# Two-layer hybrid attention block on one core: the second layer's output product as groups of seven products of sums

## The chip, the cores and the metric

The kernel runs on one core of one Trainium2 chip. The metric is the time of one execution on the device, in microseconds (us). The engines of the core are named as the profile names them: PE (TensorE, matrix products; PEld is its loading of the stationary operand, which overlaps PE), DVE (VectorE), ACT (ScalarE), POOL (GpSimd) and SP (SyncE, here only a queue that starts transfers). Every engine takes its own instructions in order and waits at one whose inputs are not there yet.

## The reference

The model has two layers (DEPTH = 2) over 512 tokens of 1024 features, with 16 meta tokens in front (T = 528). Each layer normalizes, projects, runs a sparse attention branch and a pooling branch, and joins both with gates. What matters here is the end of a layer:

```python
y_a = jnp.einsum('bte,ed->btd', attn * jax.nn.silu(gate_a), w_a)
...
y_b = jnp.einsum('bte,ed->btd', pooled * jax.nn.silu(gate_b), w_b)
g_a, g_b = jnp.split(jax.nn.sigmoid(merge), 2, axis=-1)
return x + jnp.einsum('btd,de->bte', g_a * y_a + g_b * y_b, w_out)
...
return h[:, N_META:]
```

The last line of the layer is the output product: the merged features (528 x 1024) times w_out (1024 x 1024), plus the residual x. Of the second layer only the 512 tokens behind the meta tokens are returned, so its product is 512 x 1024 x 1024.

## The kernel before

**Layout.** Activations lie features by tokens: 128 features of a stripe on the partitions, eight stripes j = 0 to 7, tokens along the free axis. Token t = 1 to 4 of the list TOK means tokens 16 to 143, 144 to 271, 272 to 399 and 400 to 527. Every float32 matrix operand is split into a high part (a cast to the reduced type float32r) and a low part (the remainder), and a product is made of three: high by high, high by low, low by high. So a cast, mostly on ACT, and a subtraction, on DVE or POOL, stand before each operand.

**Weights.** The list `chunks` (lines 114 to 131) gives the weight matrices in the order of their use, in pieces. A raw chunk is loaded by SP into two tiles (`raw`, four buffers, so two chunks lie there at a time). A plain chunk is split by `high` and `low` (lines 194 to 202): two casts of 128x1024 on ACT and two subtractions of that size on DVE. `w_load` in `low` starts the load of the next chunk, whose transfers wait for the tiles to be free.

**Groups of seven products.** The chunks named in `mixed` (lines 128 and 243 to 305) are used otherwise: ten chunks of w_in per layer in `mix_gates` (line 959). There the product of 256 output features with 1024 input features by two token halves is not eight block products but seven, of sums of blocks, by a scheme of the Strassen and Winograd kind. The weights' sums need two DVE operations of 128x512 (s2, and s2 minus a11) and two transfers on POOL's queue that add one tile to another (`first_sum` in line 239, and a12 plus s2 in line 266); after that come seven casts and seven subtractions of 128x512. The sums of the activations are made once for all ten (`sums_of_h`). Each product is 12 matmuls of 128x256. Its results are put together from PSUM banks U, S and X with copies on ACT (`out`) and sums on DVE (`total`).

**Around the output product, second layer.** First comes the attention branch's product with w_a (lines 1284 to 1304): for each stripe j, two halves of tokens, 12 matmuls each into one of three PSUM banks `d`. DVE then makes the merged value in place (`ta[j]`): one operation that multiplies the gate with the bank, which frees it, and one that adds the other branch (`zb`). ACT casts it to `hhi`, and POOL subtracts to get `hlo` (stripe 7: DVE). At the same time DVE and ACT split the first chunk of w_out.

Then comes the output product (lines 1360 to 1381): four chunks of 256 output features by four tiles of 128 tokens, sixteen groups. Each group transposes the residual `RES` (two transposes on PE, copied by ACT to `rt`), makes 24 matmuls with tokens as the rows of the result, and DVE adds half the product to `rt` and gives `ot`, which SP stores. In the very first group the three matmuls of k = 7 stand last (line 1374), since stripe 7 is the last to be ready.

**Order.** PE and DVE run in the order in which the program writes them; `later(fn, n)` puts work off until n groups of matmuls have been issued. ACT, POOL and SP are ordered by a scheduler. `prep_one` takes the next step of weight preparation from a queue, one for each group that is done.

Of the kernel before, what the change touches and what calls it, by code (L numbers as in the profile page):

```python
# [8 lines left out]
F32 = mybir.dt.float32  # L9
# [6 lines left out]
D = 1024  # L16
# [74 lines left out]
def tile_block(ctx: ExitStack, tc: tile.TileContext, x, meta, w_in, pool_w, w_a, w_b, w_out, rows, hgain, c_tab, out):  # L91
# [864 lines left out]
    ROLES = [(0, 1, 2), (2, 0, 1), (1, 2, 0)]  # L956
    NEEDS = {"a11": 2, "a12": 2, "s2": 4, "s1": 5, "s3": 6, "s4": 7, "a22": 8}

    def mix_gates(sa, zb, ta, s0, n2, operands, splits, alos):
        base = popped[0] - progress[W["use"]]  # L960
        for q in range(-2, 8):
            if q == -1:
                share[0] = FULL
            c = W["use"]
            W["use"] += 1
            ops = ready[c]
            w_prep_enqueue()
            bs = [bank("d") for _ in range(3)]
            U, S, X = (bs[r] for r in ROLES[(q + 2) % 3])
            done = [0]  # L970

            def product(ps, name, start):
                while progress[c] <= NEEDS[name]:
                    prep_one()
                B, wt = operands[name], ops[name]
                for k in range(4):
                    for e, (x, y) in enumerate(((0, 0), (0, 1), (1, 0))):
                        pe.matmul(ps[:, :n2], wt[:, x, k], B(y, k), start=start and k == e == 0,
                                  stop=k == 3 and e == 2, skip_group_check=True)

            def end():
                done[0] += 1
                group_done()
                while prep_q and (popped[0] < base + 9 * (q + 2) + LEAD + done[0] * 9 // 7 or (q == 7 and done[0] > 4)):
                    prep_one()

            def gate(eh, t, src, in_sheet):
# [20 lines left out]
                dve.tensor_tensor(o, ps[:, :n2], part, op=OP.add)  # L1008
                gate(eh, t, o, True)

            def out(ps, name):
                o = sheet(n2, name)[:, :n2]
                act.copy(o, ps[:, :n2])
                return o
# [4 lines left out]
            product(U, "a11", True)  # L1019
            p1 = out(U, "p1")  # L1020
            end()
            product(X, "a12", True)
            end()
            product(U, "s2", False)
            u = out(U, "u2")
            total(0, 0, X, p1)
            end()
            product(S, "s1", True)
            p5 = out(S, "p5")
            end()  # L1030
            if q == 7:
                alos()
            product(U, "s3", False)
            total(1, 1, U, p5)
            end()
            product(S, "s4", False)
            total(0, 1, S, u)
            end()
            product(U, "a22", False)
            gate(1, 0, U[:, :n2], False)  # L1040
            end()
            splits()
            ready.pop(c)
            if q == -1:
                later(lambda: SIL.update(ready=True), 4)


    ss0 = one.tile([128, 5], F32, name="ss0")
# [46 lines left out]
    for l in range(2):  # L1095
# [187 lines left out]
        flush()  # L1283
        for c in range(2):
            w = chunk()
            for mi in range(4):
                j = 4 * c + mi
                for hf, a, n, o in (halves if l == 0 else [(0, 16, HB - 16, 0), (1, HB, T - HB, 0)]):
                    ps = dense(w, mi, a, n, (ahi, alo), 4, True)
                    d = ta[j][:, a:a + n]  # L1290
# [66 lines left out]
                    later(lambda: norm_half(1, 0, mm, LAG2), 2)  # L1357
            hooks = {0: lambda: stats(1), 1: lambda: norm_half(1, 1, mm, LAG3)}
        else:
            for c in range(4):  # L1360
                w = chunk()
                for t in range(1, 5):
                    s, m = TOK[t]
# [15 lines left out]
                    dve.scalar_tensor_tensor(ot[:, :256], ps[:, :256], 0.5, rt[:, :256], op0=OP.mult, op1=OP.add)  # L1379
                    nc.sync.dma_start(out[0, s - 16:s + 112, c * 256:(c + 1) * 256], ot[:, :256])  # L1380
                    group_done()


# [50 lines left out]
```

## Time and profile before

| what | value |
|---|---|
| three runs | 753.22, 750.17, 749.46 us, median 750.17 |
| the profiled execution | 753.65 us |
| its span in the profile | 751.9 us |
| granted PE clock over the span | 0.999 |
| first matmul of the output product to the end of the last | 699.71 to 748.52 us |

The span is the time from the first to the last instruction of the profiled execution; the execution itself is 1.75 us longer. Rows of a timeline begin with the start in us from the span's start and the duration in us, then the engine, the line, the operation, the tiles written and read, shapes, and the count where neighbours were merged; in square brackets stands the idle time before and what ended it. Because of a helper that records costs, all PE and DVE instructions carry line 62, so they are told apart by their tiles. Rows of the chain of waits have start, duration, engine and tile. In a table by group the last columns are busy us in all, mean ns of one, and idle us before with its cause.

### The profile page before, as it was taken

What the parts mean: (1) busy time and instruction counts of PE and PEld (TensorE: products, weight loads), DVE (VectorE), ACT (ScalarE), POOL (GpSimd) and SP (SyncE); (2) the same over time, 40 slices, a digit from 0 to 9 for tenths busy, and PEclk for the clock granted to TensorE, in tenths of its full rate; (3) what the DMA queues carried; (4) which work ended last, traced back from release to release, by engine and by line L of the source; (5) the groups of instructions that cost most, each with busy time, mean ns of one, the idle gap of its engine ahead of it and who ended that gap; (6) DMA issues with size and microseconds to landing.
All of it is one profiled execution on the core that took longest, in us unless ns stands there. A gap on an engine that the chain in (4) does not pass through costs nothing.

```text
span 751.9 us, 15957 instructions
## 1 busy us (share of the span) xinstructions
PE 738.9 (98%) x5962; PEld 711.0 (95%) x5962; DVE 575.8 (77%) x1452; ACT 468.3 (62%) x1061; POOL 241.9 (32%) x312
## 2 busy tenths in 40 slices
PE   8999999999999999999999999999999999999998
PEld 7999999999999999999999989998899999999998
DVE  5876898998998865794359668999989986668531
ACT  5768745657887875543245886557588887754320
POOL 2652174621222130163256401755022221205100
PEclk9999999999999999999999999999999999999999
DMA  7666674864563444633422776669354643435411
GB/s 261 213 160 166 161 164 114 205 162 99 120 133 86 97 107 107 195 131 117 139 87 85 192 187 164 166 152 233 77 122 117 137 104 94 112 108 192 140 44 43
DMA packets 99277, 103.26 MB, mean 137 GB/s; under 512 B 4816, under 2 KB 80368, under 8 KB 99200
## 3 DMA queue, kind: packets, MB, share of 16 engines
q1 hardware_dynamic: 88752, 74.89, 32.6%
q0 software_dynamic: 10368, 27.27, 19.7%
q8 instruction: 47, 0.77, 0.4%
q14 instruction: 30, 0.25, 0.1%
q10 hardware_dynamic: 80, 0.08, 0.1%
HBM read 66.41 MB, written 8.55 MB: 100 GB/s over the span
## 4 chain that ended last, share of the span: by engine, by line
PE 85%; DVE 9%; ACT 3%; DMA 1%; issue 1%; POOL 0%; SPq 0%; DVEq 0%; POOLq 0%; ACTq 0%
PE d L62 69%; PE a L62 11%; PE v L62 4%; DVE w L62 3%; DVE lt L62 1%; DVE sc L62 1%; DVE s L62 1%; DVE c L62 1%; DMA xt<-in_x_dram 1%; DVE sila L62 1%; DMA raw<-s 1%; ACT lt L764 1%; ACT w L253 1%; DVE zb L62 1%; DVE m L62 0%
## 5 line engine op out<-in xcount | busy, mean ns | idle before, releaser
L62 PE MATMUL d<-hhi,w 128*128 128x256 f32 (+3 forms) x1344 | 268.9, 291 | 1.4 <-DVE w L62 1.4
L62 PEld LDWEIGHTS d<-hhi,w 128*128 128x128 f32 x1344 | 214.3, 188 | 5.2 <-DVE w L62 2.5
L62 PE MATMUL d<-hlo,w 128*128 128x256 f32 (+3 forms) x672 | 182.9, 289 | 0.0
L62 PEld LDWEIGHTS d<-hlo,w 128*128 128x128 f32 x672 | 126.5, 188 | 1.4 <-issue 0.2
L62 DVE TENSOR_TENSOR w<-raw,w 128x512 fp32r<-128x512 f32 (+1 forms) x152 | 123.0, 819 | 2.4 <-ACT w L253 2.2
L62 PE MATMUL d<-w,hhi 128*128 128x256 f32 x768 | 121.9, 287 | 0.3 <-ACT sq L642 0.3
L62 PEld LDWEIGHTS d<-w,hhi 128*128 128x128 f32 x768 | 104.5, 188 | 4.8 <-issue 1.6
L62 PE MATMUL d<-hsum,w 128*128 128x264 f32 (+1 forms) x720 | 96.6, 286 | 1.3 <-DVE w L62 0.9
L62 PEld LDWEIGHTS d<-hsum,w 128*128 128x128 f32 x720 | 90.0, 188 | 2.2 <-DVE w L62 1.1
L253 ACT CAST w<-raw 128x512 fp32r<-128x512 f32 x120 | 69.6, 621 | 10.0 <-DVE raw L62 6.5
L62 PE MATMUL d<-w,hlo 128*128 128x256 f32 x384 | 72.4, 281 | 0.0
L62 PEld LDWEIGHTS d<-w,hlo 128*128 128x128 f32 x384 | 57.0, 188 | 0.0
L62 DVE MATCH_REPLACE8 sc<-m,sc 128x400 f32<-128x400 f32 (+2 forms) x100 | 54.3, 549 | 0.0
L62 DVE MAX8 m<-sc 128x8 f32<-128x400 f32 (+2 forms) x100 | 52.7, 557 | 0.9
L211 POOL DMA_DIRECT2D w<-raw x32 | 29.6, 942 | 69.8 <-ACT w L210 48.1
L241 POOL DMA_DIRECT2D raw<-raw x20 | 18.0, 901 | 101.7 <-DMA raw<-in_w_in_dram 31.7
L779 POOL TENSOR_SCALAR pm<-lt,rs 128x16 f32<-128x16 f32 x48 | 29.4, 661 | 63.7 <-DVE rs L62 59.4
L764 ACT ACTIVATE lt<-lt,mn,NR 128x144 f32<-128x144 f32 (+3 forms) x64 | 42.2, 662 | 8.8 <-DVE mn L62 8.7
L62 DVE SCALAR_TENSOR_TENSOR sc<-r,wsg,sc 128x144 f32<-128x144 f32 (+3 forms) x56 | 32.4, 581 | 17.1 <-ACT r L688 14.9
L62 PE MATMUL d<-mhi,w 128*128 128x272 f32 (+2 forms) x192 | 45.3, 324 | 0.0
L1295 POOL TENSOR_TENSOR hlo<-ta,hhi 128x256 fp32r<-128x256 f32 (+1 forms) x28 | 28.2, 1021 | 45.7 <-PE d L62 33.2
L651 POOL TENSOR_TENSOR t<-t,t 128x256 f32<-128x256 f32 (+1 forms) x34 | 32.4, 954 | 27.5 <-DVE t L62 26.2
(224 smaller groups left out, 1449.9 us busy)
## 6 DMA issues: line engine op xcount, KB each, us to landing
raw<-in_w_in_dram SPq DMA_DIRECT2D x88, 256.0 KB, 3.3
raw<-in_w_in_dram SPq DMA_DIRECT2D x32, 512.0 KB, 4.2
w<-raw POOLq DMA_DIRECT2D x32, 512.0 KB, 5.4
raw<-in_w_out_dram SPq DMA_DIRECT2D x16, 512.0 KB, 3.3
raw<-raw POOLq DMA_DIRECT2D x20, 256.0 KB, 4.6
raw<-s POOLq DMA_DIRECT2D x20, 256.0 KB, 3.3
kept<-res SPq DMA_DIRECT2D x16, 264.0 KB, 3.5
res<-kept SPq DMA_DIRECT2D x16, 264.0 KB, 5.8
```

Source lines behind the costliest of these rows:

```text
L62: return fn(*a, **k)
L211: gp.dma_start(t, raws[c][s], accum_op=OP.add)
L241: gp.dma_start(raws[c][0][:, 1], raws[c][0][:, 0], accum_op=OP.add)
L253: act.copy(t[:, 0], blk[src[n]])
L651: added[0] = gp.tensor_tensor(t1[:m, :256], t1[:m, :256], t2[:m, :256], op=OP.add).ins
L764: act.activation(L[hh][:, :n], L[hh][:, :n], AF.Exp, scale=NR[:, i, h:h + 1], bias=mn[:, hh:hh + 1], accum_out=sm[:, hh:hh + 1])
L779: (gp if j < 3 else dve).tensor_scalar(pms[i][:, 2 * j + hh, :], L[hh][:, 0:16], rs[:, hh:hh + 1], None, op0=OP.mult)
L1295: pool_end = gp.tensor_sub(hlo[:, j, a:a + n], d, f(hhi[:, j, a:a + n]))
```

## The change

The first of the second layer's four output chunks stays as it was. The other three are put into `mixed` and go through groups of seven products, 256 output features by 512 tokens each, features by tokens. The body of `mix_gates` becomes a function of its own, `group_of_products`, with the same order of products.

The sums of the merged activations are made in `sums_of_merged` while the last four stripes of the w_a product are computed: for each pair (k, k + 4) `first` as soon as the loop comes to stripe 4 + k, `sums` two groups later, and `lows` and `fourth` three groups later. They work in place in `ta`, with the tiles t1 (osum1), t2 (osum2) and t3 (osum3) for the high and low parts; the low part of t1 is POOL's. The last sum takes the place of the second token half of `hhi` and `hlo` for stripes 0 to 3 (`last_high`, `last_low`), after the first output chunk has read them.

The results are added to the residual in place, features by tokens, and `turned_out` transposes each 128 features by 256 tokens to token rows, copies them on ACT and stores them, two products later.

```diff
+    mixed |= set(range(len(chunks) - 3, len(chunks)))
...
             if s == 1:
                 del raws[c]
                 w_load()
+                first_sum(c + 1)
...
+    def group_of_products(r, base, n2, operands, total, direct, mid=None):
...
+        product(U, "a11", True)
+        p1 = out(U, "p1")
+        end()
+        product(X, "a12", True)
+        end()
+        product(U, "s2", False)
+        u = out(U, "u2")
+        total(0, 0, X, p1)
+        end()
+        product(S, "s1", True)
+        p5 = out(S, "p5")
+        end()
+        if mid:
+            mid()
+        product(U, "s3", False)
+        total(1, 1, U, p5)
+        end()
+        product(S, "s4", False)
+        total(0, 1, S, u)
+        end()
+        product(U, "a22", False)
+        direct(1, 0, U[:, :n2])
+        end()
+        ready.pop(c)
...
+    def sums_of_merged(ta):
+
+        c0, c1 = slice(16, 272), slice(272, 528)
+        t1 = one.tile([128, 2, 4, 256], F32R, tag="D", name="osum1")
...
+        def first(k):
+            a0, a1 = ta[k][:, c0], ta[k][:, c1]
+            dve.tensor_tensor(a0, a0, a1, op=OP.subtract)
+            act.copy(t1[:, 0, k], a0)
+            gp.tensor_sub(t1[:, 1, k], a0, f(t1[:, 0, k]))
+
+        def sums(k):
+            a0, a1, b1 = ta[k][:, c0], ta[k][:, c1], ta[4 + k][:, c1]
+            dve.tensor_tensor(a1, b1, a1, op=OP.subtract)
+            dve.scalar_tensor_tensor(b1, b1, -1.0, a0, op0=OP.mult, op1=OP.subtract)
+            act.copy(t2[k][:, 0], b1)
+            act.copy(t3[k][:, 0], a1)
+
+        def lows(k):
+            dve.tensor_sub(t2[k][:, 1], ta[4 + k][:, c1], f(t2[k][:, 0]))
+            dve.tensor_sub(t3[k][:, 1], ta[k][:, c1], f(t3[k][:, 0]))
+
+        def fourth(k):
+            b0, b1 = ta[4 + k][:, c0], ta[4 + k][:, c1]
+            dve.scalar_tensor_tensor(b0, b1, -1.0, b0, op0=OP.mult, op1=OP.subtract)
+
+        def last_high(k):
+            act.copy(hhi[:, k, c1], ta[4 + k][:, c0])
+
+        def last_low(k):
+            dve.tensor_sub(hlo[:, k, c1], ta[4 + k][:, c0], f(hhi[:, k, c1]))
...
+    def turned_out(j, t):
+
+        tp = bank("a")
+        for a in range(2):
+            s = 16 + 256 * t + 128 * a
+            pe.transpose(tp[:, 128 * a:128 * a + 128], RES[0][:, j, s:s + 128], ident)
+        ot = tmp.tile([128, HB], F32, tag="tt", name="ot", bufs=6)
+        act.copy(ot[:, :256], tp[:, :256])
+        nc.sync.dma_start(out[0, 256 * t:256 * t + 256, 128 * j:128 * j + 128].rearrange("(a p) e -> p a e", a=2),
+                          ot[:, :256].rearrange("p (a e) -> p a e", a=2))
+
+    def mix_out(operands):
+        base = popped[0] - progress[W["use"]]
+        for q in range(3):
+            def add(eh, t, src):
+                j = 2 + 2 * q + eh
+                d = RES[0][:, j, 16 + 256 * t:272 + 256 * t]
+                dve.scalar_tensor_tensor(d, src, -0.5 if eh else 0.5, d, op0=OP.mult, op1=OP.add)
+                later(lambda: turned_out(j, t), 2)
+
+            def total(eh, t, ps, part):
+                o = sheet(256, "c")[:, :256]
+                dve.tensor_tensor(o, ps[:, :256], part, op=OP.add)
+                add(eh, t, o)
+
+            group_of_products(q, base, 256, operands, total, add)
+        flush()
...
             w = chunk()
+            if l and c:
+                first, sums, lows, fourth, last_high, last_low, operands = sums_of_merged(ta)
             for mi in range(4):
                 j = 4 * c + mi
+                if l and c:
+                    first(mi)
+                    later(lambda k=mi: sums(k), 2)
+                    later(lambda k=mi: (lows(k), fourth(k)), 3)
...
-            for c in range(4):
+            for c in range(1):
                 w = chunk()
...
+            for k in range(4):
+                last_high(k)
+            later(lambda: [last_low(k) for k in range(4)], 1)
+            mix_out(operands)
```

More of the change, by code (lines that the diff above doesn't have):

```diff
@@ L957, in tile_block, with product, end, out @@
     NEEDS = {"a11": 2, "a12": 2, "s2": 4, "s1": 5, "s3": 6, "s4": 7, "a22": 8}
+    def group_of_products(r, base, n2, operands, total, direct, mid=None):
+        c = W["use"]
+        W["use"] += 1
+        ops = ready[c]
+        w_prep_enqueue()
+        bs = [bank("d") for _ in range(3)]
+        U, S, X = (bs[i] for i in ROLES[r % 3])
+        done = [0]
+        def product(ps, name, start):
+            while progress[c] <= NEEDS[name]:
+                prep_one()
+            B, wt = operands[name], ops[name]
+            for k in range(4):
+                for e, (x, y) in enumerate(((0, 0), (0, 1), (1, 0))):
+                    pe.matmul(ps[:, :n2], wt[:, x, k], B(y, k), start=start and k == e == 0,
+                              stop=k == 3 and e == 2, skip_group_check=True)
+        def end():
+            done[0] += 1
+            group_done()
+            while prep_q and (popped[0] < base + 9 * r + LEAD + done[0] * 9 // 7 or (mid and done[0] > 4)):
+                prep_one()
+        def out(ps, name):
+            o = sheet(n2, name)[:, :n2]
+            act.copy(o, ps[:, :n2])
+            return o
+        product(U, "a11", True)
[22 more added lines that the diff above has]
+        ready.pop(c)
     def mix_gates(sa, zb, ta, s0, n2, operands, splits, alos):
@@ L963, in mix_gates, with gate @@
                 share[0] = FULL
[L964 to L987, printed above, removed]
+            def gate(eh, t, src, in_sheet=False):
                 j = 2 * q + eh
@@ L1018, in mix_gates @@
                     ta[j] = tmp.tile([128, T], F32, tag="B", name="ta", bufs=8)
[L1019 to L1041, printed above, removed]
+            group_of_products(q + 2, base, n2, operands, total, gate, alos if q == 7 else None)
             splits()
-            ready.pop(c)
             if q == -1:
                 later(lambda: SIL.update(ready=True), 4)
+    def sums_of_merged(ta):
+        c0, c1 = slice(16, 272), slice(272, 528)
+        t1 = one.tile([128, 2, 4, 256], F32R, tag="D", name="osum1")
+        t2 = [tmp.tile([128, 4, 128], F32R, tag="P", name="osum2", bufs=PB).rearrange("p (s a) c -> p s (a c)", s=2)
+              for _ in range(4)]
+        t3 = [tmp.tile([128, 544], F32R, tag="L", name="osum3", bufs=LB)[:, :512].rearrange("p (s c) -> p s c", s=2)
+              for _ in range(4)]
+        def first(k):
[19 more added lines that the diff above has]
+            dve.tensor_sub(hlo[:, k, c1], ta[4 + k][:, c0], f(hhi[:, k, c1]))
+        operands = {
+            "a11": lambda s, k: H[s][:, k, c0],
+            "a12": lambda s, k: H[s][:, 4 + k, c0],
+            "s4": lambda s, k: H[s][:, 4 + k, c1],
+            "s1": lambda s, k: t1[:, s, k],
+            "s2": lambda s, k: t2[k][:, s],
+            "s3": lambda s, k: t3[k][:, s],
+            "a22": lambda s, k: H[s][:, k, c1],
+        }
+        return first, sums, lows, fourth, last_high, last_low, operands
```

5 lines of the change are left out of this document (1 added, 4 removed).

## The prediction

> **What bounds the kernel now.** I read the page's busy shares first, then its chain, then the chain in order of time over the last 75 us, then the windows and the timelines of VectorE (DVE) and GpSimd (POOL) there.
>
> ```profile
> span 751.9 us, 15957 instructions
> PE 738.9 (98%) x5962; PEld 711.0 (95%) x5962; DVE 575.8 (77%) x1452; ACT 468.3 (62%) x1061; POOL 241.9 (32%) x312
> PE 85%; DVE 9%; ACT 3%; DMA 1%; issue 1%; POOL 0%; SPq 0%; DVEq 0%; POOLq 0%; ACTq 0%
> ```
>
> ```profile
> 647.68 2.85 PE d L62 x24
> ...
> 677.22 22.28 PE d L62 x186
> 699.49 0.22 PE a L62 x2
> 699.71 2.84 PE d L62 x24
> 748.52 0.04 DVEq L62
> ```
>
> TensorE (PE) is the bound. From 677.22 us the chain is PE without a gap: the branch product (w_a) to 699.49, then sixteen groups of the output product, each a pair of transposes (0.22) and 24 matmuls (2.84, so 0.118 each), to 748.52. A matmul taken out saves its 0.118 as long as nothing makes PE wait. The same rate holds in the existing groups of products (24 in 2.85 at 647.68).
>
> ```profile
> 690.00:700.00 10.00, 10.00 (x87) 10.00 (x86) 8.93 (x16) 4.79 (x9) 7.60 (x8) 1.00 0.27 91
> 720.00:730.00 10.00, 10.00 (x87) 10.00 (x86) 2.41 (x4) 2.17 (x4) 0.00 (x0) 1.00 0.12 41
> 740.00:752.00 12.00, 8.51 (x73) 8.29 (x71) 1.27 (x3) 0.74 (x2) 0.00 (x0) 0.94 0.13 45
> ```
>
> The columns are the window, its length, busy time of PE, weight loads, DVE, ACT and POOL, the granted clock, and DMA. Here lies the difficulty. The output product has DVE and POOL nearly free (DVE 2.41 of 10 us), but the new sums start ahead of it, in the second half of the branch product, where DVE is busy 8.93 of 10 us and POOL 7.60.
>
> **The change part by part.** *Matmuls.* Removed are 12 groups of 24 = 288; added are three chunks of seven products of 12 = 252. The 36 fewer are worth 36 x 0.118 = **-4.26 us**. The 24 transposes of these chunks stay, behind the products instead of ahead. Six 128x1024 subtractions on DVE and six casts on ACT go too; they were hidden (2.41 and 2.17 of 10 us busy) and give nothing.
>
> *Sums for the operands.* The merged features lie in eight stripes, j = 0 to 7. For each of four pairs (k and k + 4) DVE gets seven operations of 128x256 with both inputs in SBUF: first 1, sums 2, lows 2, fourth 1, and last_low 1 later. By the order of the instructions eleven of them (four first, two sums pairs, one lows pair, one fourth) come ahead of the update of stripe 7, and DVE takes its queue in order.
>
> ```profile
> 683.65 1.21 DVE L62 TENSOR_TENSOR w<-raw,w 128x1024 fp32r<-128x1024 f32 x1
> 686.12 0.42 DVE L62 TENSOR_TENSOR ta<-ta,zb 128x256 f32<-128x256 f32 x1
> 686.46 1.76 DVE L62 TENSOR_TENSOR w<-raw,w 128x1024 fp32r<-128x1024 f32 x1
> ...
> 691.01 0.42 DVE L62 SCALAR_TENSOR_TENSOR ta<-ta,d 128x256 f32<-128x256 f32 x1 [0.22 <-PE d L62]
> 691.47 0.90 DVE L62 TENSOR_TENSOR ta<-ta,zb 128x256 f32<-128x256 f32 x1
> ...
> 693.85 0.42 DVE L62 SCALAR_TENSOR_TENSOR ta<-ta,d 128x256 f32<-128x256 f32 x1 [0.54 <-PE d L62]
> ...
> 700.75 0.43 DVE L62 TENSOR_TENSOR hlo<-ta,hhi 128x256 fp32r<-128x256 f32 x1 [0.47 <-ACT hhi L1293]
> 701.09 0.41 DVE L62 SCALAR_TENSOR_TENSOR ta<-ta,d 128x256 f32<-128x256 f32 x1
> ...
> 702.77 0.42 DVE L62 SCALAR_TENSOR_TENSOR ot<-d,rt 128x256 f32<-128x256 f32 x1
> ```
>
> ```profile
> 682.71 0.74 POOL L1295 TENSOR_TENSOR hlo<-ta,hhi 128x256 fp32r<-128x256 f32 x1 [0.80 <-ACT hhi L1293]
> 684.25 1.22 POOL L1295 TENSOR_TENSOR hlo<-ta,hhi 128x256 fp32r<-128x256 f32 x1 [0.80 <-ACT hhi L1293]
> 686.26 2.56 POOL L1295 TENSOR_TENSOR hlo<-ta,hhi 128x256 fp32r<-128x256 f32 x2 [0.80 <-ACT hhi L1293]
> 689.63 2.45 POOL L1295 TENSOR_TENSOR hlo<-ta,hhi 128x256 fp32r<-128x256 f32 x3 [0.81 <-PE d L62]
> ```
>
> A short DVE operation holds its place for 0.34 us (686.12 to 686.46). Beside POOL it takes up to 0.90 instead of 0.42, 0.48 more; the 128x1024 subtraction takes 1.76 instead of 1.21, and POOL's 0.74 becomes 1.22: DVE and POOL hold each other up. The change puts four more subtractions (osum1) on POOL, three of them ahead of the hlo row of stripe 7 (700.75).
>
> The row that matters is hlo of stripe 7, first half. It starts at 700.75 and ends at 701.17. PE reads it as third of the last three matmuls of the first output group: 699.71 + 23 x 0.118 = 702.43, so there is 1.26 us of cover. The eleven cost 11 x 0.34 = 3.74. Three added POOL operations, each waited out at 0.74, cost 2.2. The idle 0.22 + 0.54 in the rows gives 0.76 back. So the row ends 5.2 later, at 706.35, and PE waits 5.2 - 1.26 = **+3.9**. Low end: no POOL wait, 3.74 - 0.76 - 1.26 = 1.7. High end: all eleven meet POOL at 0.48, 11 x 0.82 - 0.76 - 1.26 = 7.0. I take 3.9, because POOL is busy three quarters of that stretch and only some updates there show the longer time. Part of the wait appears earlier: the last half stripe of the branch product waits for a d bank that DVE has not read, and the output group's fifth k step for the low half of its weights.
>
> The Trainium skill's page "SBUF — State Buffer", section "Who interferes with whom", says that a VectorE instruction with two SBUF inputs and a GpSimd instruction that reads SBUF exclude each other for the whole instruction, whoever starts first. The 1.22, 1.76 and 0.90 above agree with that; if by this rule all eleven waited out a full POOL operation, the wait would be 11 x 1.08 - 2.0 = 9.9 and the sum +7.3, against +1.3 by the rows' mix.
>
> *Queues passed.* Ahead of eight of POOL's fourteen subtractions now stands the trigger that adds a11 to a21 of the first chunk, which waits for that chunk's first load.
>
> ```profile
> L241 POOL DMA_DIRECT2D raw<-raw x20: 852/887/1227, 153.3 to 638.6; - x20
> ```
>
> ```profile
> DMA to landing us min/median/max: 3.3/4.1/5.3
> ```
>
> The load's slot frees with the DVE subtraction of 683.65, at 684.86, so it lands by 688.2 to 690.2, when POOL has just reached that place (2.56 from 686.26). The gap before its next row, 0.81, takes most of the trigger's 0.9: nothing more in the sum. At the late end POOL's rows start some 1.5 later, hlo of stripe 4 is late, and the sums on DVE wait for it: the high end above. SP issues twelve half-size loads in place of six, with the stores between and behind them; it has nothing else left to do. POOL's two triggers a group stand before nothing but the next trigger.
>
> *Entering the groups.* Behind the last hlo DVE has 13 short operations, three ot and three half-chunk operations (a12 low, s2, a11 low) before PE's next product.
>
> ```profile
> L62 DVE TENSOR_TENSOR w<-raw,w 128x512 fp32r<-128x512 f32 x120 | 80.9, 684 | 2.4 <-ACT w L253 2.2
> L253 ACT CAST w<-raw 128x512 fp32r<-128x512 f32 x120 | 69.6, 621 | 10.0 <-DVE raw L62 6.5 <-DMA raw<-s 2.6 <-PE d L62 0.5
> PE d L62 <- DVE w L62: 2.5, 5, 0.9
> ```
>
> From 706.35 + 1.7 (the rows from 701.09 to 702.77) that is 13 x 0.34 + 3 x 0.42 + 3 x 0.68, so 715.8. PE ends the fourth output group at 706.5 + 3 x 3.06 = 715.7 and needs a11's low part two matmuls later: **+0.3**, between 0 and 1.0, the ends by how far DVE trails.
>
> *Inside the groups.* For each, DVE has nine operations of 0.68 and seven of 0.42, 9.1 us, and ACT seven casts of 0.62 and seven copies of 0.37 (the rt row below), 6.9 us, beside 84 x 0.118 + 4 x 0.22 = 10.8 us of PE. So they are hidden; uncovered, the wait would be the longest in the table, 0.9, once or twice a group. The twenty present groups carry at most the 2.5 us above, 0.13 each: **+0.4**. ACT's sixteen new casts of sums fall where it is busy 4.79 or less of 10.
>
> *The end.* Before, after the last matmul come ot and its store. Now come the residual sum on DVE (as long), then transposes, a copy, the store.
>
> ```profile
> 705.36 0.24 PEld L62 LDWEIGHTS a<-consts,res 128*128 128x128 f32 x2
> 705.46 0.38 PE L62 MATMUL a<-consts,res 128*128 128x128 f32 x2
> 705.88 0.37 ACT L1370 COPY rt<-a 128x256 f32<-128x256 f32 x1 [2.65 <-PE a L62]
> ```
>
> ```profile
> DMA to landing us min/median/max: 1.7/1.7/2.0
> ```
>
> From 705.36 to the copy's end is 0.89; with two hand-overs of about 0.05 **+1.0**. Low end 0.8; high end 1.3, if the store in half-length rows lands at the longest 2.0.
>
> *Sum.* -4.26 + 3.9 + 0.3 + 0.4 + 1.0 = **+1.3 us**. The profiled execution took 753.65 around its span of 751.9 and would become 755.0 (span 753.2). It lies 3.5 above the median of 750.17, which becomes **751.5**.
>
> **The rivals.** *The cover holds.* DVE and POOL hardly collide: 1.7 in place of 3.9, entry 0, end 0.8: -4.26 + 1.7 + 0.4 + 0.8 = -1.4, 748.8; with no wait at the first output group, 747.1. For it: DVE is idle from 702.77 on for most of each group. Against: the eleven stand before that point.
>
> *DVE and POOL in lockstep: slower.* The sums of the pairs with stripes 4 and 5 wait for POOL's hlo of the same stripe, and POOL, with 11 subtractions and a trigger in that stretch, runs each at 1.22. At the upper bounds, 7.0 of wait, 1.0 at the entry and 1.3 at the end: +5.4, 755.6. Behind a waiting sum in DVE's queue stand its reads of the d banks, and PE waits for those. It decides once the hlo row ends after 709, against 706.35: 2.6 more carries the time over 753.9. For it: 2.56 for two POOL rows. Against: POOL also ran three in a row at 0.82 (2.45 from 689.63).
>
> *Operands late in the groups.* One or two waits of 0.9 a group, 2.7 to 5.4 instead of 0.4: 753.8 to 756.5. Against it: 9.1 of 10.8 us.
>
> *The clock falls behind the wait.* If PE, idle for some us, came back at half rate for one group of 24, 2.84 more: 754.3. Every window above but the last shows 1.00, and the last, in which PE ends, 0.94. The Trainium skill's page "TensorE: Matmul & The Clock Gate", Part 1, has the clock halve after an idle window of about 3.4 us; no run here yet shows such a wait.
>
> **How the numbers follow.** My forecast (749.5 to 753.9) has 0.49, the held cover 0.18, lockstep 0.20, late operands 0.08, the clock 0.05. About 0.5%, 3.75 us, is what a measurement here tells from no change: 746.4 and 753.9. The last three give slower 0.33. None reaches 746.4, even without waits (747.1); the spread of the runs shown (749.46 to 753.22) leaves 0.07 of the held cover to faster. Same has 0.60. The range runs from 747.0 (no wait) to 756.0 (lockstep, and late operands nearly to their end).
>
> **What would show it.** Right: the span's PE has about 36 x 0.118 less work; the first output group shows PE waiting some 4 us in all, put down to DVE w, hlo or ACT hhi; short DVE operations there of 0.6 to 0.9; almost no waits inside the three groups; an end of PE, DVE, PE, ACT, store about 1 us longer. Wrong: that group without waits (cover held), hlo past 709 (lockstep), DVE or POOL waits in every group, or a granted clock under 1.00 behind the wait.

## The result, and the profile after

| what | before | after |
|---|---|---|
| median of 19 runs each, taken on the same chip | 751.05 us | 753.70 us |
| ratio, with its 95% interval | | 1.0044 (1.0033 to 1.0056) |
| the profiled execution and its span | 753.65, 751.9 us | 754.19, 752.4 us |
| granted clock over the span | 0.999 | 0.995 |

By the ratio the changed kernel is 3.3 us slower; the two medians of all runs lie 2.65 us apart. The page of its profile, the lines that answer to those of before:

```profile
span 752.4 us, 16023 instructions
PE 735.7 (98%) x5926; PEld 706.9 (94%) x5926; DVE 601.9 (80%) x1510; ACT 482.4 (64%) x1101; POOL 249.8 (33%) x322
PE 86%; DVE 9%; ACT 3%; issue 1%; DMA 1%; POOL 1%; SPq 0%; DVEq 0%; POOLq 0%; ACTq 0%
```

36 matmuls fewer, PE 3.2 us less busy, and yet no gain. The spans differ by 0.5 only because the two profiled executions part earlier than the change: the w_a product starts at 676.13 before and at 673.14 after, with nothing edited ahead of it. So all that follows is counted from that start. First the rows of before, then those of after (timeline of PE, with the idle time in brackets).

```profile
676.13 0.87 PE L62 MATMUL d<-ahi,w 128*128 128x256 f32 x6
...
711.60 0.38 PE L62 MATMUL a<-consts,res 128*128 128x128 f32 x2
```

```profile
673.14 0.87 PE L62 MATMUL d<-ahi,w 128*128 128x256 f32 x6
...
696.87 1.21 PE L62 MATMUL d<-ahi,w 128*128 128x256 f32 x8 [1.60 <-DVE ta L62]
...
702.30 0.39 PE L62 MATMUL d<-w,hhi 128*128 128x256 f32 x1 [1.98 <-DVE w L62]
...
703.86 0.74 PE L62 MATMUL d<-w,hhi 128*128 128x256 f32 x2 [0.33 <-ACT hhi L1381]
...
715.11 0.28 PE L62 MATMUL d<-hhi,w 128*128 128x256 f32 x1
```

The end of the first output chunk (711.60 before, 715.11 after) lies 35.47 and 41.97 us behind the start: **6.50 lost**. From there to the end of the span it is 40.30 and 37.29: **3.01 gained**. Together 75.77 and 79.26 us, 3.49 more, close to the 3.3 of the timed runs. Up to the end of the first output chunk PE has three waits that the kernel before hasn't, 3.91 us of idle time in all. What the chain of waits shows of after, in order of time:

```profile
674.23 5.18 PE d L62 x42
...
679.43 0.43 DVE ta L62
...
702.95 0.43 DVE ta L62
...
703.40 0.41 ACT hhi L1381
...
703.86 1.04 PE d L62 x3
...
705.33 3.81 PE d L62 x24
...
709.36 2.86 PE d L62 x24
...
712.43 8.50 PE d L62 x72
```

Before, PE alone carried the chain from 677.22 on. Now DVE carries it from 679.43 to 703.38, a cast of ACT follows (hhi), and the groups of products behind run 72 matmuls in a row (8.50 / 72 = 0.118 each). Between them stands a surprise: the second output group takes 3.81 in place of 2.84. The windows say why (columns as above; the last is the stretch of that group):

```profile
690.00:700.00 10.00, 8.40 (x71) 8.19 (x70) 9.72 (x18) 5.04 (x12) 7.36 (x9) 1.00 0.19 54
720.00:730.00 10.00, 9.93 (x84) 9.69 (x84) 7.71 (x16) 4.87 (x12) 1.71 (x2) 1.00 0.84 210
```

```profile
703.60:707.00 3.40, 3.14 (x14) 3.13 (x15) 2.65 (x8) 0.61 (x2) 0.36 (x1) 0.55 0.50 145
```

DVE is busy 9.72 of 10 us beside the branch product, and behind the waits the granted clock is 0.55 for 3.4 us. DVE's timeline, the sums (ta<-ta, osum) and the row that matters, with two rows of POOL:

```profile
686.82 2.12 DVE L62 TENSOR_TENSOR ta<-ta 128x256 f32<-128x256 f32 x1
...
690.53 0.95 DVE L62 TENSOR_TENSOR ta<-ta 128x256 f32<-128x256 f32 x1
...
693.18 0.95 DVE L62 TENSOR_TENSOR ta<-ta 128x256 f32<-128x256 f32 x1
694.24 0.78 DVE L62 SCALAR_TENSOR_TENSOR ta<-ta 128x256 f32<-128x256 f32 x1
...
698.07 1.84 DVE L62 TENSOR_TENSOR osum<-ta,osum 128x256 fp32r<-128x256 f32 x2
...
703.84 0.43 DVE L62 TENSOR_TENSOR hlo<-ta,hhi 128x256 fp32r<-128x256 f32 x1 [0.47 <-ACT hhi L1381]
```

```profile
686.31 0.88 POOL L243 DMA_DIRECT2D raw<-raw  x1 [0.48 <-DMA raw<-in_w_out_dram]
686.93 1.72 POOL L1383 TENSOR_TENSOR hlo<-ta,hhi 128x256 fp32r<-128x256 f32 x2
```

A sum that takes 0.42 elsewhere takes 0.95 beside POOL, and the first one 2.12: it ends at 688.94, POOL's two subtractions at 688.65. Six of the eleven sums are lengthened, by 4.2 us in all (0.75 is what two in a row take otherwise); the other five take 0.41 to 0.42. The hlo row of stripe 7 stands 30.70 us behind the start (703.84), against 24.62 before: 6.08 later.

### The profile page after: what moved, and what is told of

Read it like the earlier page. It is cut to its first block, busy times and chain, and to the rows that moved or that the text cites. A ratio compares the mean times of both kernels' runs of the same rounds, so it can differ in the third digit from the quotient of the medians.

```text
span 752.4 us, 16023 instructions
## 1 busy us (share of the span) xinstructions
PE 735.7 (98%) x5926; PEld 706.9 (94%) x5926; DVE 601.9 (80%) x1510; ACT 482.4 (64%) x1101; POOL 249.8 (33%) x322
## 4 chain that ended last, share of the span: by engine, by line
PE 86%; DVE 9%; ACT 3%; issue 1%; DMA 1%; POOL 1%; SPq 0%; DVEq 0%; POOLq 0%; ACTq 0%
PE d L62 70%; PE a L62 12%; PE v L62 4%; DVE w L62 3%; DVE ta L62 2%; DVE lt L62 1%; DMA xt<-in_x_dram 1%; DVE s L62 0%; DVE c L62 0%; ACT lt L766 0%; DVE sc L62 0%; DVE raw L62 0%; ACT w L255 0%; DVE zb L62 0%; ACT w L212 0%
## 5 line engine op out<-in xcount | busy, mean ns | idle before, releaser
L62 PE MATMUL d<-hhi,w 128*128 128x256 f32 (+3 forms) x1440 | 288.4, 291 | 1.4 <-DVE w L62 1.4
L62 PEld LDWEIGHTS d<-hhi,w 128*128 128x128 f32 x1440 | 229.9, 188 | 5.3 <-DVE w L62 2.4
L62 PE MATMUL d<-hlo,w 128*128 128x256 f32 (+3 forms) x720 | 196.4, 288 | 0.0
L62 PEld LDWEIGHTS d<-hlo,w 128*128 128x128 f32 x720 | 135.6, 188 | 1.4 <-issue 0.2
L62 PE MATMUL d<-w,hhi 128*128 128x256 f32 x576 | 88.0, 290 | 2.6 <-DVE w L62 2.0
L255 ACT CAST w<-raw 128x512 fp32r<-128x512 f32 x138 | 79.7, 621 | 10.4 <-DVE raw L62 7.2
L62 PEld LDWEIGHTS d<-w,hhi 128*128 128x128 f32 x576 | 76.3, 191 | 7.5 <-DVE w L62 2.2
L268 POOL DMA_DIRECT2D raw<-s x23 | 20.1, 872 | 83.0 <-DVE c L62 33.9
L62 PE MATMUL d<-w,hlo 128*128 128x256 f32 x288 | 46.1, 283 | 0.0
L62 DVE TENSOR_TENSOR c<-d,p 128x256 f32<-128x256 f32 (+1 forms) x38 | 16.1, 423 | 32.3 <-PE d L62 25.8
```

The source lines that it names most:

```text
L62: return fn(*a, **k)
L255: act.copy(t[:, 0], blk[src[n]])
L268: gp.dma_start(blk["a12"], blk["s2"], accum_op=OP.add)
```

## The experiments

Theory: eleven sums ahead of stripe 7's update, lengthened by POOL, make PE wait, and the clock falls behind the wait; the products themselves save 3 us. Rivals: the groups of products cost the time; the number of sums alone does, or POOL's added work alone. The table counts from the start of the w_a product, in us, in one profiled execution of each; each ratio is to runs of the kernel before on the same chip.

| kernel | ratio to before, interval | hlo row | end of first output chunk | end of span |
|---|---|---|---|---|
| before | | 24.62 | 35.47 | 75.77 |
| changed | 1.0044 (1.0033, 1.0056) | 30.70 | 41.97 | 79.26 |
| changed, second look | 1.0032 (1.0018, 1.0046) | 30.75 | 41.94 | 79.29 |
| products alone | 0.9967 (0.9955, 0.9979) | 25.11 | 35.46 | 72.86 |
| t1's low part on DVE | 1.0043 (1.0029, 1.0057) | 31.00 | 40.86 | 79.02 |
| three sums later | 1.0032 (1.0021, 1.0043) | 29.59 | 39.46 | 78.21 |
| trigger behind | 1.0027 (1.0013, 1.0041) | 29.67 | 40.25 | 77.59 |
| no POOL subtractions | 0.9991 (0.9977, 1.0006) | 26.82 | 36.72 | 74.47 |
| all sums behind | 1.0014 (1.0004, 1.0023) | 25.01 | 35.47 | 76.38 |
| the same, reordered | 1.0004 (0.9989, 1.0018) | 24.77 | 35.13 | 75.69 |
| sums spread | 1.0051 (1.0038, 1.0064) | 29.10 | 38.98 | 78.42 |
| two chunks | 0.9968 (0.9953, 0.9984) | 24.54 | 35.14 | 73.78 |
| PE filled at both places | 1.0100 (1.0087, 1.0114) | 30.54 | 40.43 | 83.45 |
| PE filled at the second place | 1.0049 (1.0031, 1.0068) | 29.76 | 39.62 | 77.44 |

**Products alone.** Is it the groups or the sums?

```diff
-                    first(mi)
-                    later(lambda k=mi: sums(k), 2)
-                    later(lambda k=mi: (lows(k), fourth(k)), 3)
...
-            "s1": lambda s, k: t1[:, s, k],
-            "s2": lambda s, k: t2[k][:, s],
-            "s3": lambda s, k: t3[k][:, s],
+            "s1": lambda s, k: H[s][:, k, c0],
+            "s2": lambda s, k: H[s][:, 4 + k, c1],
+            "s3": lambda s, k: H[s][:, k, c1],
```

> The changed kernel without the 28 sums of the merged features on DVE, their 16 casts on ACT and the 4 subtractions on POOL; the products of sums read the plain stripes of hhi and hlo instead, so the sums are left out of the result. Theory (the loss is DVE's queue ahead of the last stripe): no wait of PE at the first output group beyond what the kernel before has, granted clock 1.00 from 700 us on, and the time is before -4.26 (36 matmuls) +0.4 (inside the groups) +1.0 (end) = -2.9 us, ratio 0.996. Rival (the groups of products themselves cost it, by late operands, transposes or their end): not below the kernel before, ratio 1.000 to 1.004.

75.77 became 72.86, -2.91, where -2.9 was expected. From the w_a product on PE waits for DVE's w once, 0.2, as before, and once for res at the end. The groups pay for themselves; the sums, with their casts and POOL's four subtractions, which this kernel leaves out as well, cost the rest.

**More sums on DVE, fewer on POOL.**

```diff
-            gp.tensor_sub(t1[:, 1, k], a0, f(t1[:, 0, k]))
...
         def lows(k):
+            dve.tensor_sub(t1[:, 1, k], ta[k][:, c0], f(t1[:, 0, k]))
```

> The changed kernel with the low part of t1 (4 subtractions) on DVE, behind the casts, in lows(k), in place of POOL. Ahead of the last stripe's update stand twelve sums on DVE in place of eleven, and three subtractions fewer on POOL. Theory A (the sums are lengthened by POOL's subtractions, which exclude DVE's): short DVE operations there drop from 0.8 to 0.95 us to 0.42, the wait of PE shrinks by 1 to 2.5 us and the time is 1 to 2.5 us under the changed kernel, ratio to the kernel before 1.001 to 1.003. Theory B (only the number of operations on DVE counts): one more of 0.34 us, ratio 1.0045 to 1.005.

```profile
684.59 2.31 DVE L62 TENSOR_TENSOR ta<-ta 128x256 f32<-128x256 f32 x1
...
688.40 0.96 DVE L62 TENSOR_TENSOR ta<-ta 128x256 f32<-128x256 f32 x1
```

These rows of DVE's timeline are as long as in the changed kernel, and hlo stands 0.30 later, one operation's place. Theory B: the four subtractions that the change gave to POOL were not what lengthened the sums. Here the clock stayed at 1.00, so this run also measures the waits alone: idle 1.50 + 2.23 + 0.35 = 4.08 by the rows, and the output chunk 5.39 later. So a wait costs some 0.4 more than its idle time. Some 0.27 of that is in the rows of PE: a row of one matmul lasts 0.28 although the next one starts 0.118 behind it where nothing waits, so 0.16 of each wait lies inside the row ahead of it; and the first matmul behind the wait holds its place for 0.23 (702.30 to 702.53 in the changed kernel) in place of 0.118. The rest is not accounted for. (In four of this kernel's six timed executions the mean granted clock is 0.995 or 0.997, so there it fell too.)

**Fewer sums ahead.**

```diff
-                    later(lambda k=mi: (lows(k), fourth(k)), 3)
+                    later(lambda k=mi: (lows(k), fourth(k)), 3 if mi else 4)
```

> The changed kernel with lows and fourth of the first pair (three operations on DVE) behind the update of the last stripe: eight sums ahead of it in place of eleven. Theory A (each sum ahead of it costs its place in DVE's queue, 0.34 alone to 0.72 beside POOL): the fourth output group ends 1.0 to 2.2 us earlier against the start of the w_a product than in the changed kernel (45.15 us from that start there), ratio 1.0015 to 1.003. Rival (the first sum's 2.12 us and the 128x1024 subtractions set the wait, not the number of sums): less than 0.5 us earlier, ratio 1.004.

(The 45.15 there is mis-subtracted; the changed kernel's row stands at 41.97.) The chunk ended 2.51 earlier, 1.2 of it without the clock, which stayed at 1.00 (see below), so a sum ahead costs 0.4 on the mean: theory A by the chunk, while the ratio, 1.0032, lies just above its range. The rows of PE's timeline:

```profile
699.84 0.39 PE L62 MATMUL d<-w,hhi 128*128 128x256 f32 x1 [0.80 <-DVE w L62]
...
712.71 0.51 PE L62 MATMUL d<-hhi,w 128*128 128x256 f32 x2 [1.06 <-DVE w L62]
```

The wait for w is 0.80 in place of 1.98; but 1.06 came back as a wait where the first group of products is entered, since DVE is still behind there.

**POOL's trigger.**

```diff
-                first_sum(c + 1)
+                if c < len(chunks) - 4:
+                    first_sum(c + 1)
...
+        if l:
+            with tc.issue_after(pool_end.ins):
+                first_sum(len(chunks) - 3)
```

> The changed kernel with POOL's trigger for the first chunk of products (a11 added to a21) behind its last subtraction of hlo, in place of ahead of eight of them. Theory B (the trigger's 0.88 us and the two subtractions that it delays hold up DVE's first sum, which took 2.12 us in place of 0.42): the first sum takes at most 1.0 us, the fourth output group ends 0.9 to 1.5 us earlier against the start of the w_a product, ratio 1.0025 to 1.0035. Rival (the gap in POOL's queue hides the trigger and DVE is filled up anyway): less than 0.4 us earlier, ratio 1.004 to 1.005.

```profile
686.70 0.96 DVE L62 TENSOR_TENSOR ta<-ta 128x256 f32<-128x256 f32 x1
```

The first sum takes 0.96 in place of 2.12, hlo comes 1.03 earlier and the chunk 1.72 earlier, 1.67 over the whole tail: theory B, by a little more than it said. Only the 1.03 is the sum's: the clock fell here too (behind a wait of 1.99), but 0.7 less was lost by it, since the slow matmuls ran while hhi was still to come, and PE has no wait for it in this run.

**POOL's subtractions.**

```diff
-                    if j < KT - 1:
+                    if l and j < KT - 1:
+                        act.copy(hlo[:, j, a:a + n], d)
+                    elif j < KT - 1:
...
-            gp.tensor_sub(t1[:, 1, k], a0, f(t1[:, 0, k]))
+            act.copy(t1[:, 1, k], a0)
```

> The changed kernel with POOL's 14 subtractions of hlo (stripes 0 to 6) and 4 of t1 in the second layer taken away: ACT writes a copy of the merged value there instead, so the low parts are left out. The eleven sums stand on DVE where the change put them. Theory A (POOL's subtractions and DVE's operations with two SBUF inputs exclude each other, and that makes a sum take 0.5 to 1.0 us in place of 0.34): all sums show 0.42, eleven take 3.7 us, less than DVE's idle gaps, cover and the collisions that the kernel before has too; PE waits at most 1.0 us up to the end of the first output group, ratio 0.996 to 0.998. Theory B (eleven operations ahead of the last stripe are too many, POOL or not): a wait of 1.7 to 3 us, ratio 0.9985 to 1.001. Rival (ACT's or PE's part): as the changed kernel, 1.004.

```profile
685.01 0.42 DVE L62 TENSOR_TENSOR ta<-ta 128x256 f32<-128x256 f32 x1
...
691.14 0.43 DVE L62 SCALAR_TENSOR_TENSOR ta<-ta 128x256 f32<-128x256 f32 x1
...
694.53 0.75 DVE L62 TENSOR_TENSOR osum<-ta,osum 128x256 fp32r<-128x256 f32 x2
```

Every sum takes 0.42, two in a row 0.75, and with the eleven in the same place the chunk ends 1.25 later than in the kernel before, in place of 6.50 us. The two remaining waits are 0.46 and 0.35. By the rows that is theory A: POOL's subtractions, the old ones of hlo among them, are what the sums run into. But the ratio, 0.9991, lies in the range of theory B, and its interval only touches that of A. Nor is 1.25 the price of eleven sums alone: without POOL's subtractions DVE's other operations get shorter too (none of 0.90 or 1.76 as in the kernel before), and the kernel before without them was not run. What the Trainium skill's page "SBUF — State Buffer", section "Who interferes with whom", says of two-input operations agrees with this pair of runs (0.95 and 2.12 with POOL, 0.42 without).

**The sums behind the last stripe.**

```diff
-                    first(mi)
-                    later(lambda k=mi: sums(k), 2)
-                    later(lambda k=mi: (lows(k), fourth(k)), 3)
...
+        if l:
+            for k in range(4):
+                first(k)
+            for k in range(4):
+                sums(k)
+            later(lambda: [lows(k) for k in range(4)], 1)
+            later(lambda: [t1_low(k) for k in range(4)], 5)
+            later(lambda: [(t3_low(k), fourth(k)) for k in range(4)], 8)
+            later(lambda: [last_high(k) for k in range(4)], 9)
+            later(lambda: [last_low(k) for k in range(4)], 10)
```

> The changed kernel with all sums issued behind the update of the last stripe, on DVE alone: first and the two sums of all pairs before the first ot, the low parts and the fourth sums spread over the first output chunk and the first group of products. Theory (the place of the sums costs it): no wait of PE at the first output group, no clock loss, at most 1 us of waits where the first group of products is entered: -2.9 to -1.9 us against the kernel before, ratio 0.996 to 0.9975. Rival (DVE's work has to be done anyway, so the wait moves to the entry of the groups): waits of 3 to 5 us at a11, s2 or s1 of the first group and a ratio of 1.001 to 1.004.

```profile
713.52 3.05 PE L62 MATMUL d<-osum,w 128*128 128x256 f32 x24 [1.48 <-ACT p L988]
...
721.57 0.39 PE L62 MATMUL d<-hlo,w 128*128 128x256 f32 x1 [1.60 <-DVE hlo L62]
```

The first output chunk has its old 35.47, as the theory said, but 3.1 us came back as waits in the first group of products, at s2, where the rival had them, and at a22. The time is the rival's. ACT's copy p stood behind casts that wait, and DVE, busy 4.65 to 4.96 of every 5 us from 700 to 725, came late with hlo. So p was put ahead and the order changed.

```diff
+            with tc.issue_after(W["p1"]) if "p1" in W else nullcontext():
+                act.copy(t[:, 0], blk[src[n]])
...
+            later(lambda: [fourth(k) for k in range(4)], 6)
+            later(lambda: [(t3_low(k), last_high(k)) for k in range(4)], 7)
+            later(lambda: [last_low(k) for k in range(4)], 8)
```

> All sums behind the last stripe as in the run before with three chunks of products, with ACT's copy p of the first group of products ordered ahead of the casts that stood in front of it, the fourth sums and the last subtractions of hlo moved ahead of the weight preparation of the next chunk. Theory (the 1.48 us for p were ACT's order, the 1.60 us for hlo are DVE's work that does not fit in 15 us): the wait for p goes, that for hlo stays between 1 and 2 us: 74.3 to 75.3 us from the start of the w_a product to the end, ratio 0.998 to 0.9995. Rival (PE only runs into DVE earlier, and the sum of the waits stays 3.3 us): 76.2 to 76.6 us, ratio 1.001.

0.69 came off, where the theory had 1.1 to 2.1. The waits for p and hlo are gone; PE now waits ahead of two pairs of transposes (0.53 and 1.34), the second pair starting as DVE's residual sum ends. The time is that of the kernel before, and neither side's: DVE, busy 4.66 to 4.97 of every 5 us from 700 to 720, does not get through all of it beside one output chunk.

**The sums spread.** first and the low part of t1 went beside the first half of the w_a product:

```diff
+                if l and c == 0:
+                    later(lambda k=mi: first(k), 1)
+                    later(lambda k=mi: t1_low(k), 2)
```

> The changed kernel with the sums spread: first and the low part of t1 (on DVE) already in the first half of the w_a product, two groups behind their stripe, where DVE has idle gaps of 0.3 to 0.5 us per half stripe; the two sums of every pair and all that follows behind the update of the last stripe; ACT's copy p of the first group of products ordered ahead of the casts that the scheduler put before it. Behind the last stripe DVE has 8 operations fewer than with all sums behind (2.7 us), so the two waits left there (1.48 for p, 1.60 for hlo) should go. Theory (only the place of the sums costs it): -2.9 to -1.7 us against the kernel before, ratio 0.996 to 0.998, no wait above 0.5 us. Rival (DVE is full from 680 us on, whatever the order, and every order pays): waits of 2 to 4 us in all, ratio 0.999 to 1.002.

```profile
686.56 0.96 DVE L62 TENSOR_TENSOR osum<-ta,osum 128x256 fp32r<-128x256 f32 x1
687.45 0.95 DVE L62 TENSOR_TENSOR ta<-ta 128x256 f32<-128x256 f32 x1
```

No better than the changed kernel, and the rival's waits, 3.3 us in all (its ratio, 1.0051, is above what the rival said): of these eight all but the first take 0.95 to 0.97, and with 0.89 from one start to the next they fill some 6.6 us of DVE's queue, not 2.7. POOL's subtractions of hlo run beside them (two from 686.37 on, 1.74 together, beside the two rows shown), so the gaps that DVE's timeline had before were not free for them.

**Two chunks.** Eight plain groups of 3.06 us have room for all sums:

```diff
-    mixed |= set(range(len(chunks) - 3, len(chunks)))
+    mixed |= set(range(len(chunks) - 2, len(chunks)))
...
+            for k in range(4):
+                later(lambda k=k: (first(k), sums(k)), 1 + k)
+                later(lambda k=k: (lows(k), fourth(k)), 3 + k)
```

> Two output chunks stay as before and two go through groups of products; all sums, the low part of t1 too, stand on DVE behind the update of the last stripe, one pair behind each of the first four of eight output groups. Theory (the place of the sums costs it, and behind the last stripe a sum takes 0.34 us, so 8 output groups of 3.06 us hold all of them): no wait of PE above 0.3 us; two thirds of the gain, -2.84, +1.0 at the end, +0.2 at the transposes: -1.6 us against the kernel before, ratio 0.9975 to 0.9985, and 74.1 us from the start of the w_a product to the end (before 75.77). Rival (the groups' own waits at their entry come wherever they begin): 0.5 to 1.5 us of waits at the entry, ratio 0.999 to 1.001.

```profile
700.00:724.00 24.00, 24.00 (x204) 23.85 (x203) 20.80 (x49) 13.32 (x33) 1.71 (x2) 1.00 0.39 105
```

PE doesn't stop in the 24 us in which DVE does the sums; 73.78 in place of 75.77. By the ratio this version is 0.32% faster than the kernel before (0.16 to 0.47; the medians lie 1.37 us apart), and it is the fastest of those that leave nothing out.

**The clock.** Matmuls whose result nothing reads fill PE's waits, first at both places:

```diff
+                        for e in range(12):
+                            pe.matmul(spare_bank[:, :256], w[0][0][:, :128], ahi[:, 0, 16:272], start=True, stop=True)
...
+                        if t == 1 and e == 12:
+                            for _ in range(15):
+                                pe.matmul(spare_bank[:, :256], hhi[:, 0, 16:144], w[0][0], start=True, stop=True)
```

> The changed kernel with 12 matmuls of 128x256 ahead of the last half stripe of the w_a product and 15 ahead of the fifth k step of the first output group, into a spare PSUM bank from operands that are there already; nothing reads their result. They stand where PE waits 1.60 and 1.98 us and take 12 x 0.118 = 1.4 and 15 x 0.118 = 1.8 us. Theory (the idle stretches make the granted clock fall, and the half clock costs 1.5 us of the loss): granted clock 1.00 throughout, 1.2 to 1.7 us under the changed kernel, ratio to the kernel before 1.002 to 1.003. Rival (the clock costs nothing, since PE would wait for DVE anyway): the same as the changed kernel or up to 0.5 us above it, ratio 1.004 to 1.005.

```profile
717.88 1.66 ACT L255 CAST w<-raw 128x512 fp32r<-128x512 f32 x3 [2.46 <-DMA raw<-s]
719.44 0.36 ACT L988 COPY p<-d 128x256 f32<-128x256 f32 x1
```

```profile
719.85 4.38 PE L62 MATMUL d<-osum,w 128*128 128x256 f32 x23 [3.76 <-ACT p L988]
```

```profile
720.00:723.40 3.40, 3.40 (x18) 3.40 (x19) 1.88 (x4) 0.69 (x2) 0.85 (x1) 0.56 0.28 67
```

Failed as a test: the scheduler put ACT's copy p behind three casts that wait for a transfer, and a wait of 3.76 arose (ratio 1.0100, 1.0087 to 1.0114). It shows the fall once more: clock 0.56 for 3.4 us. Then twelve at the second place alone, with ACT's order kept:

> The changed kernel with 12 matmuls of 128x256 ahead of the fifth k step of the first output group alone, into a spare PSUM bank; nothing reads their result, and ACT's order stays that of the changed kernel. They take 1.42 of the 1.98 us that PE waits there. Theory (the idle stretch makes the granted clock fall for the next 3.4 us): granted clock 1.00 in the stretch behind, the second output group takes 3.05 us in place of 3.81 + 0.43, and from the first matmul of the w_a product to the end the profile shows 1.3 to 1.7 us less than the changed kernel's 79.26; ratio to the kernel before 1.002 to 1.0035 if the clock falls in most executions. Rival (the clock falls whatever PE does there, or costs nothing): 79.0 to 79.6 us and 1.004 to 1.005.

```profile
705.00:710.00 5.00, 4.66 (x37) 4.50 (x38) 3.83 (x11) 1.68 (x5) 0.44 (x1) 1.00 0.35 104
```

The clock stayed at 1.00, and the span ended 77.44 behind the start, 1.82 less. The chunk ended 2.35 earlier, and 0.94 of that isn't the filling: hlo came so much earlier, as the first sum took 1.05 here in place of 2.12. In five of this kernel's six timed executions the mean granted clock is 1.000, in the changed kernel in one of 27: that the filling keeps the clock up is shown. What it is worth in the median is not settled by it: the ratio is 1.0049 (1.0031 to 1.0068), not lower, and the six times scatter from 751.79 to 756.02. The front of the kernel, in which nothing was changed, scatters as well: the w_a product starts between 670.88 and 676.13 in the profiled executions, here at 675.56. So the changed kernel was looked at again:

> The changed kernel once more, unedited, for a second profile. If the granted clock falls behind the 2 us wait in every execution: the second output group again takes more than 3.5 us and 79.0 to 79.5 us pass from the start of the w_a product to the end. If it falls only where the wait meets the clock's windows: a second output group of 3.05 us, granted clock 1.00, and 77.4 to 78.0 us. Ratio to the kernel before 1.003 to 1.0055 in either case.

```profile
702.00:705.40 3.40, 3.05 (x15) 2.85 (x15) 2.42 (x8) 0.81 (x2) 0.68 (x1) 0.58 0.54 154
```

It fell again, and the end came at 79.29. What one fall costs can be read from PE's timelines: from the end of the wait for hhi to the transposes of the third output group it is 5.12 us in the changed kernel (703.86 to 708.98) and 5.04 here, but 3.73 with t1's low part on DVE and 3.74 with the filling, so 1.3 to 1.4 a fall. How often it falls can be read from the mean granted clock of each timed execution: 3.4 us at half rate take 0.5 x 3.4 / 752 = 0.002 from it. Of 27 executions of the changed kernel 7 show 0.995, 19 show 0.997 or 0.998 and one 1.000, so 33 falls, 1.2 each. Of the 78 of the kernel before that ran beside the experiments 31 show 0.997 or 0.998 and none less: 0.4 each, and without this wait. In these executions of the kernel before, the median with a fall is 1.1 to 1.8 us above the median without, in each of the four sets of runs. So about 0.8 falls more at 1.4: an estimate of **1.1 us** of the 3.3.

## Why the prediction was right, and where its sum was off

The case that was called likeliest came: +0.44% is within the 0.5%, and 753.7 is in the range. It came narrowly, with an interval that reaches +0.56%. The sum was off by more than its own size: it said +1.3, and it is +3.3:

| step | predicted | measured |
|---|---|---|
| 36 matmuls | -4.26 | -4.26 (72 in 8.50 behind) |
| wait at the first output group | +3.9 | 6.50 - 1.3 = +5.2 |
| clock behind the wait | a rival, 2.84 | +1.3 in this execution, some 1.1 in the median |
| entering the groups | +0.3 | 0 |
| inside the groups | +0.4 | +0.3 |
| the end | +1.0 | +1.0 |

(The 1.3 is what is left of 6.50 when the idle 3.91 and the 1.31 that the run with t1's low part on DVE showed beside its idle time are taken off; the timelines above give 1.3 to 1.4 directly; the last three rows make -3.01 with the first.)

*The mis-sized term is the wait.* Its place, its releasers (DVE w, ta, ACT hhi) and its mechanism came as said, hlo 6.08 later against 5.2. But its working laid the price of POOL on the three subtractions added there, 2.2 us, where the rows show sums lengthened by 4.2. The run with them on DVE shows that they cost next to nothing; the run without POOL's subtractions shows that those which POOL had before, too, are what the sums run into. And the trigger on POOL's queue was priced at nothing since a gap of 0.81 would take it: moving it away gave 1.0 on the hlo row. Without POOL's subtractions the chunk ends 1.25 later; the prediction's low bound, with no wait for POOL, was 1.7. The lockstep rival's point wasn't reached: with 2.99 for the different start the hlo row ended at 704.27 + 2.99 = 707.26, against 706.35 predicted and 709 from which that rival decides.

*The clock was no rival but a term.* A granted clock under 1.00 behind the wait was one of the prediction's own signs of being wrong, and it came. It got 0.05 as a case of its own at the price of a whole group at half rate; it comes on top of the wait, in most executions, at about half that price: half rate for 3.4 us loses at most 1.7. Wait and clock together lie 2.6 above what the sum had for them, and the entry and the groups give back 0.4: that the time was still no more than 0.5% (3.75 us) above the kernel before is owed to the room up to that bound, not to the size of the terms.

*The groups* were right in all: the entry without a wait, no operand late, and the end:

```profile
748.05 0.42 DVE L62 SCALAR_TENSOR_TENSOR res<-d,res 128x256 f32<-128x256 f32 x1 [0.75 <-PE d L62]
```

```profile
748.53 0.44 PE L62 MATMUL a<-consts,res 128*128 128x128 f32 x2 [0.30 <-DVE res L62]
```

```profile
749.00 0.37 ACT L1108 COPY ot<-a 128x256 f32<-128x256 f32 x1 [0.36 <-PE a L62]
```

From 748.53 to the copy's end at 749.37 is 0.84, which the kernel before hasn't; the predicted piece was 0.89.

## What to carry to other kernels

An engine that idles a few tenths beside each tile isn't free for new work, if the new work is held up by another engine's: here an operation that holds its place for 0.34 cost 0.9 beside POOL's subtractions and 0.34 where POOL was idle. Work that only a later product needs is best not put ahead of the last operand of the next one; here two chunks of products with room behind for their sums beat three with the sums crowded in. And a wait of 2 us may cost more than 2 us: here a stretch at half clock stood behind it in most executions, 1.3 to 1.4 us.

## What was not expected of the hardware

In the profiled executions the granted clock fell to about half for some 3.4 us behind waits of 1.98, 2.00, 1.99 and 3.76 us, and didn't behind 2.23 in the run with t1's low part on DVE, nor behind 1.68 and 0.80 in that with three sums later. The Trainium skill's page "TensorE: Matmul & The Clock Gate", Part 1, asks for an idle window of about 3.4 us: the length of the slow stretch agrees, the wait that brings it about was shorter. It may be that a fixed window need only be idle for the most part, and that 2 us do or don't fill it by where it begins; no run here tells.

DVE's first sum took 1.93 to 2.31 us in five of the runs with the trigger ahead of POOL's subtractions, 1.05 in a sixth (PE filled at the second place), and 0.96 with the trigger behind them. The trigger alone doesn't lengthen a sum: beside the changed kernel's second trigger (POOL, 700.44, 0.87) a sum took 0.42 (700.68), and with the trigger behind, three beside the two triggers (698.41, 1.75) took 0.41 to 0.42. The long sums end 0.3 behind the two subtractions that follow the trigger; why a sum waits out both of them there and only one elsewhere, no run here tells.
